# A layer norm taken in centred form: output weights and residual less their means

## The chip, the cores and the metric

The kernel runs on one core of a Trainium2 chip. The metric is the device time of one execution, in microseconds (us); the number that counts is the median over runs.

## The reference, cut to what matters

One post-norm decoder layer over 256 tokens and 1024 channels. Four mixers (Mamba-2 SSD, HGRN2, retention, block-sparse attention) of 256 channels each fill `y_cat`; one projection leads back to 1024 channels, and a layer norm with weight and bias ends it.

```python
def _layernorm(x, g, b):
    xf = x.astype(F32)
    mu = jnp.mean(xf, -1, keepdims=True)
    var = jnp.mean(jnp.square(xf - mu), -1, keepdims=True)
    return ((xf - mu) * lax.rsqrt(var + LN_EPS) * g + b).astype(x.dtype)
...
    y_cat = jnp.concatenate([y_ssd, y_hgrn, y_ret, y_moba], axis=-1).astype(x.dtype)
    y = jnp.einsum('blm,md->bld', y_cat, w_out)
    return _layernorm(DEEPNORM_ALPHA * x + y, ln_g, ln_b)
```

All of it is float32; the change touches only the last two lines.

## The kernel before, in words

**Tiles.** 256 tokens are two tiles of 128 (T = 0, 1). The contraction over 1024 channels is eight tiles of 128. Every matmul runs in a split form: a float32 operand is taken apart into a high part (rounded to the matmul's type) and a low part (the rest), and three products are added up: high by high, low by high, high by low. For weights `split_hi` (L225) makes the high part `whi` by a cast on ACT and `split_lo` (L234) the low part `wlo` by a subtraction on DVE.

**Slots.** The work is written by hand as a row of slots. Slots 0 to 29 are the input projections (`project`), two slots for a unit of 256 columns or for half of a pair of units. At slot s `begin(s)` starts the load of weight half s+6 (five buffers `raw`, all loads on SP's queue, in order), makes the high part of half s+4 on ACT, runs the steps that the table `steps` lists for that slot, and makes the low part of half s+4 on DVE. Every engine works its own instructions strictly in the order in which they are written. So ACT's and DVE's queues hold the weight splits between the mixers' steps.

**Output projection.** `w_out` is loaded as four blocks of 256 rows, each in two halves j of 512 columns (`wr_wo`; i = NU + 0 to 3, NU = 15, with `ORDER` = 0, 3, 1, 2: SSD, attention, HGRN2, retention). They are split in slots 26 to 33, four slots ahead of use. `oproj(i, T, c0, c1)` (L992 to L994) adds one block into a PSUM bank `po`. Its left side is `yhi`, `ylo`, the split of the transposed mixer outputs, made by `y_split` (L436 on ACT, L437 on DVE) and, for attention, L896 and L897. The order on PE: block 0 and block 1 for T = 0, the transposes of HGRN2 and retention (slot 32, L431), block 0 for T = 1, blocks 2 and 3 for T = 0, and at the end blocks 1 to 3 for T = 1, column piece by column piece. T = 0 has two pieces of 512 columns, T = 1 pieces of 512, 256, 256 (`OCOLS`).

**Slots 26 to 33 hold more than splits.** ACT makes the attention gate (`moba_out`, L894) and its `yhi`, the two SiLU gates of HGRN2 and retention from the last projection (`gates`, L630, slot 30) and the two `yhi` copies after the transposes (slot 32). POOL makes the retention norm's inverse root (`rsqrt_of`, L255 and L256: a multiply-add and a power).

**Residual.** `residual(T)` (slots 21, 22; L977, L978) puts alpha times the normalized input, with weight and bias, into `xn[T]`, on DVE. It reads the row vectors `rb`, whose one buffer is loaded again for the last norm's weight and bias once both residuals are through; SP issues the later weight loads behind that load.

**Last norm.** When a piece of `po` is complete, `out_add` adds it into `xn` (L1000) and takes statistics of the piece (L1001). After the last piece `out_norm` joins the statistics (L1006), has POOL make the inverse root (L255, L256), meanwhile subtracts the mean and multiplies by the weight (L1011), then multiplies by the root, adds the bias (L1014), and SP stores the pieces.

Of the kernel before, what the change touches and what calls it, by code (L numbers as in the profile page):

```python
# [122 lines left out]
def hybrid_layer(  # L123
# [21 lines left out]
    def sb(shape, name, tag=None, dt=F32, bufs=1):  # L145
        return sp.tile(shape, dt, name=name, tag=tag or name, bufs=bufs)
# [24 lines left out]
    mhalf = cp.tile([P, 8], F32, name="mhalf")  # L171
    nc.gpsimd.memset(mhalf, -0.5)


# [794 lines left out]
    def load_rows(first):  # L969
# [3 lines left out]
        rowt[first] = t  # L973

    def residual(T):
        rb = rowt[0]
        nc.vector.scalar_tensor_tensor(xn[T], xn[T], ALPHA, rb[:, 0, :], op0=ALU.mult, op1=ALU.mult)  # L977
        nc.vector.scalar_tensor_tensor(xn[T], rb[:, 1, :], ALPHA, xn[T], op0=ALU.mult, op1=ALU.add)  # L978

# [15 lines left out]

    fst = [sb([P, len(OCOLS[T]) - 1, 6], f"fst{T}") for T in range(NT)]

    def out_add(T, n):
        cs = slice(OCOLS[T][n], OCOLS[T][n + 1])
        nc.vector.tensor_add(xn[T][:, cs], xn[T][:, cs], po[T, cs.start])  # L1000
        nc.vector.bn_stats(fst[T][:, n, :], xn[T][:, cs])  # L1001

    def out_norm(T):
        rb = rowt[2]
        m_ = sb([P, 2], f"fmv{T}")
        nc.vector.bn_aggr(m_, fst[T])  # L1006
        rs = sb([P, 1], f"frs{T}")
        rsqrt_of(rs, m_[:, 1:2], 1.0, LN_EPS)
        cuts = [slice(a, b) for a, b in zip(OCOLS[T], OCOLS[T][1:])]
        for cs in (slice(0, 512), slice(512, 1024)):  # L1010
            nc.vector.scalar_tensor_tensor(xn[T][:, cs], xn[T][:, cs], m_[:, 0:1], rb[:, 0, cs],  # L1011
                                           op0=ALU.subtract, op1=ALU.mult)
        for cs in cuts:
            nc.vector.scalar_tensor_tensor(xn[T][:, cs], xn[T][:, cs], rs[:, 0:1], rb[:, 1, cs],  # L1014
                                           op0=ALU.mult, op1=ALU.add)
            nc.sync.dma_start(out[T * P:(T + 1) * P, cs], xn[T][:, cs])
# [45 lines left out]
    def begin(slot):  # L1062
        if slot < 32:
            load_w(*divmod(slot + 6, 2))
        if slot < 34:
            split_hi(*divmod(slot + 4, 2))
        for st in steps.get(slot, []):
            st()
        if slot < 34:
            split_lo(*divmod(slot + 4, 2))  # L1070

    first_unit()
# [62 lines left out]
```

## Time and profile before

| | us |
|---|---|
| median of 3 runs (lowest to highest) | 150.19 (150.09 to 150.38) |
| the profiled execution | 150.68 |
| its span, first to last instruction | 149.0 |
| PE busy, 1224 matmuls | 137.5 |
| DVE busy, 240 instructions | 116.5 |
| ACT busy, 122 instructions | 75.0 |
| POOL busy, 23 instructions | 17.8 |

The span is what the trace covers; 1.68 us of the profiled execution lie outside it. A busy share is a mean over stages with different limits, so it only says where to look first. The chain that ended last tells at each moment which instruction was waited for; an engine's timeline tells what ended its idle time (in brackets, with the releaser). The mean granted clock of TensorE was 0.971.

### The profile page before, as it was taken

Reading aid. Unit: us, or ns where it says so; the run is one execution under the profiler, and the core shown is the slowest. Engines: PE = TensorE matmul, PEld = TensorE weight load, DVE = VectorE, ACT = ScalarE, POOL = GpSimd, SP = SyncE. Lnnn points to the kernel's source line nnn. Section 1 sums busy time; section 2 is a strip of 40 time slices with the busy share of each in tenths; the row PEclk is TensorE's granted clock in tenths of the full one; section 3 lists DMA queues with packets and bytes.
Section 4 is the critical chain, followed back from the end, with each engine's and each line's share of the span. In section 5 each row is a group of like instructions: output and inputs, shape, how many; then the busy total and the mean of one; then the engine's idle time right before and its main releaser. Section 6 shows DMA issues by size and latency. Waiting matters only on the chain.

```text
span 149.0 us, 3073 instructions
## 1 busy us (share of the span) xinstructions
PE 137.5 (92%) x1224; PEld 122.5 (82%) x1224; DVE 116.5 (78%) x240; ACT 75.0 (50%) x122; POOL 17.8 (12%) x23
## 2 busy tenths in 40 slices
PE   5869999999999999999999999999999999999800
PEld 3149999999999998878899999999888888888800
DVE  1789968999596297969997599976989975478681
ACT  3088969742451759599709970054954635000000
POOL 4230000000000000000062018014004000004040
PEclk9996999999999999999999999999999999999975
DMA  4998399998748431595524830179774530000304
GB/s 141 328 384 312 95 292 342 324 319 317 201 139 258 136 60 80 148 272 165 163 101 145 306 119 4 35 232 383 243 239 141 159 127 0 0 0 0 141 0 141
DMA packets 9389, 26.05 MB, mean 175 GB/s; under 512 B 1056, under 2 KB 1696, under 8 KB 9120
## 3 DMA queue, kind: packets, MB, share of 16 engines
q1 hardware_dynamic: 9376, 25.87, 53.3%
q8 instruction: 9, 0.15, 0.4%
q14 instruction: 4, 0.03, 0.1%
HBM read 24.82 MB, written 1.05 MB: 174 GB/s over the span
## 4 chain that ended last, share of the span: by engine, by line
PE 81%; DVE 7%; DMA 3%; ACT 2%; SPq 1%; issue 1%; POOLq 1%; POOL 1%; DVEq 0%
PE pj_gg L381 8%; PE po L993 5%; PE po L994 5%; PE po L992 5%; PE pj_h_f L346 5%; PE pj_xs L420 4%; PE pj_m_k L420 4%; PE pj_m_g L420 4%; PE pj_r_k L420 4%; PE pj_m_q L420 4%; PE pj_h_i L420 4%; PE pj_zv L381 4%; PE pj_h_q L420 4%; PE pj_r_v L420 4%; PE pj_r_q L420 4%; DMA wr_h_f<-in_w_dram 3%
## 5 line engine op out<-in xcount | busy, mean ns | idle before, releaser
L992 PE MATMUL po<-whi_wo,yhi 128*128 128x512 f32 (+1 forms) x40 | 14.0, 350 | 0.0
L993 PE MATMUL po<-wlo_wo,yhi 128*128 128x512 f32 (+1 forms) x40 | 14.0, 349 | 0.0
L994 PE MATMUL po<-whi_wo,ylo 128*128 128x512 f32 (+1 forms) x40 | 13.9, 348 | 0.0
L234 DVE TENSOR_TENSOR wlo_wo<-wr_wo,whi_wo 128x1024 fp32r<-128x1024 f32 x8 | 9.6, 1219 | 0.0
L225 ACT CAST whi_wo<-wr_wo 128x1024 fp32r<-128x1024 f32 x8 | 8.2, 1050 | 2.3 <-PE pj_gg L381 1.7
L710 POOL TENSOR_SCALAR_AFFINE_SELECT ra<-ahi 128x1024 fp32r<-128x1024 f32 x1 | 1.1, 1101 | 65.0 <-DVE ahi L706 65.0
L992 PEld LDWEIGHTS po<-whi_wo,yhi 128*128 128x128 f32 x40 | 7.5, 188 | 1.1
L994 PEld LDWEIGHTS po<-whi_wo,ylo 128*128 128x128 f32 x40 | 7.5, 188 | 1.0
L993 PEld LDWEIGHTS po<-wlo_wo,yhi 128*128 128x128 f32 x40 | 7.5, 188 | 1.0
L225 ACT CAST whi_zv<-wr_zv 128x1024 fp32r<-128x1024 f32 x4 | 4.2, 1048 | 6.8 <-PE pj_xs L420 3.4
L179 PE MATMUL warm<-warm 128*128 128x512 f32 x6 | 5.5, 1088 | 1.5 <-DVE warm L176 1.5
L656 DVE SCALAR_TENSOR_TENSOR cacc_xs<-pj_xs,ch,cacc_xs 128x255 f32<-128x255 f32 (+2 forms) x6 | 2.9, 482 | 4.7 <-ACT cacc_xs L654 4.6
L381 PE MATMUL pj_zv<-whi_zv,hhi 128*128 128x512 f32 x16 | 6.5, 406 | 0.0
L381 PE MATMUL pj_gg<-whi_gg,hhi 128*128 128x512 f32 x16 | 6.4, 398 | 0.0
L1000 DVE TENSOR_TENSOR xn<-xn,po 128x512 f32<-128x512 f32 (+1 forms) x5 | 2.9, 580 | 4.4 <-PE po L994 4.4
L381 PE MATMUL pj_zv<-whi_zv,hlo 128*128 128x512 f32 x16 | 6.3, 394 | 0.0
L381 PE MATMUL pj_gg<-whi_gg,hlo 128*128 128x512 f32 x16 | 6.3, 394 | 0.0
L381 PE MATMUL pj_zv<-wlo_zv,hhi 128*128 128x512 f32 x16 | 6.3, 392 | 0.0
L381 PE MATMUL pj_gg<-wlo_gg,hhi 128*128 128x512 f32 x16 | 6.3, 392 | 0.0
L225 ACT CAST whi_gg<-wr_gg 128x1024 fp32r<-128x1024 f32 x4 | 4.2, 1046 | 2.5 <-DMA wr_gg<-in_w_dram 1.7
L793 ACT ACTIVATE ssq<-sy 128x512 f32<-128x512 f32 x1 | 0.6, 631 | 9.0 <-DVE sy L791 9.0
L860 ACT ACTIVATE pe<-pe,mmax 128x128 f32<-128x128 f32 (+1 forms) x8 | 3.5, 445 | 3.0 <-DVE mmax L853 3.0
(281 smaller groups left out, 494.1 us busy)
## 6 DMA issues: line engine op xcount, KB each, us to landing
wr_wo<-in_wo_dram SPq DMA_DIRECT2D x8, 512.0 KB, 3.9
wr_zv<-in_w_dram SPq DMA_DIRECT2D x4, 512.0 KB, 4.5
rb<-in_rows_dram SPq DMA_DIRECT2D x2, 1024.0 KB, 6.5
wr_gg<-in_w_dram SPq DMA_DIRECT2D x4, 512.0 KB, 4.9
wr_h_i<-in_w_dram SPq DMA_DIRECT2D x2, 520.0 KB, 5.3
xt<-in_x_dram SPq DMA_DIRECT2D x4, 256.0 KB, 3.7
wr_h_f<-in_w_dram SPq DMA_DIRECT2D x4, 256.0 KB, 5.0
wr_h_q<-in_w_dram SPq DMA_DIRECT2D x2, 512.0 KB, 6.7
```

The lines of the kernel that those rows point to most:

```text
L179: nc.tensor.matmul(wb, warm[:, :P], warm, start=True, stop=True)
L225: copy(whi[i, j][:, r, :], t[:, r, :])
L234: nc.vector.tensor_sub(wlo[i, j][:, r, :], t[:, r, :], whi[i, j][:, r, :].bitcast(F32))
L346: nc.tensor.matmul(ps[n], l[:, n * P:(n + 1) * P], r[:, k, :], start=(k == 0 and q == 0), stop=(k == KT - 1 and q == 2))
L381: nc.tensor.matmul(ps_of[name, T], l[:, k, ts], r, start=(k == 0 and q == 0), stop=(k == KT - 1 and q == 2))
L420: nc.tensor.matmul(ps, l, r, start=(n == 0), stop=(n == len(seq) - 1))
L656: nc.vector.scalar_tensor_tensor(a_[:, d:], ps[:, :SEQ - d], tap(3 - d), a_[:, d:], op0=ALU.mult, op1=ALU.add)
L860: nc.scalar.activation(pt[:, h, :], pt[:, h, :], AF.Exp, bias=mmax[:, i:i + 1], accum_out=msum[:, i:i + 1])
L992: nc.tensor.matmul(po[T, c0], yhi[:, k, ts], hi, start=(i == 0 and j == 0), stop=False)
L993: nc.tensor.matmul(po[T, c0], yhi[:, k, ts], lo, start=False, stop=False)
L994: nc.tensor.matmul(po[T, c0], ylo[:, k, ts], hi, start=False, stop=(i == 3 and j == 1))
L1000: nc.vector.tensor_add(xn[T][:, cs], xn[T][:, cs], po[T, cs.start])
```

## The change

The mean over the 1024 output channels of alpha x + y is taken out of the inputs of the sum. Each row of `w_out` (one input channel, one partition) gets its mean over the 1024 columns subtracted before it is split, and the residual gets its own row mean subtracted. The sum then has row mean zero. The variance is the mean of squares, and the weight can be applied before the inverse root is known.

- `residual(T)`: the second instruction also gives its row sum; a one-column multiply on DVE; ACT adds the negative mean to the whole row.
- `wo_sum`, in the place of `split_hi` for the output weights: ACT copies each of a half's two row tiles in place, for the accumulator's row sum (two passes of 512 columns).
- `wo_mean`, after the second half of a block: POOL adds the two halves' sums and multiplies by -1/1024.
- `wo_split`, in odd slots after the steps, for both halves at once: ACT makes the high parts with the mean as bias (four passes of 512), DVE the low parts (four instructions).
- `out_add`: after the add ACT squares the piece, with an accumulator, and writes the squares over the spent bank; DVE multiplies the piece by the weight into `zg` and joins the piece's sum to the variance.
- `out_norm`: one POOL power, then the last multiply-add from `zg`.

```diff
--- before.py
+++ after.py
@@ -170,6 +170,8 @@
 
     mhalf = cp.tile([P, 8], F32, name="mhalf")
     nc.gpsimd.memset(mhalf, -0.5)
+    epsln = cp.tile([P, 1], F32, name="epsln")
+    nc.gpsimd.memset(epsln, LN_EPS)
 
 
     warm = sb([P, 512], "warm", tag="att")
@@ -972,10 +974,43 @@
         nc.sync.dma_start(t, rows[:, o:o + 2 * DM].to_broadcast([P, 2 * DM]))
         rowt[first] = t
 
+
+
     def residual(T):
         rb = rowt[0]
         nc.vector.scalar_tensor_tensor(xn[T], xn[T], ALPHA, rb[:, 0, :], op0=ALU.mult, op1=ALU.mult)
-        nc.vector.scalar_tensor_tensor(xn[T], rb[:, 1, :], ALPHA, xn[T], op0=ALU.mult, op1=ALU.add)
+        sm_ = sb([P, 1], f"rsum{T}")
+        nc.vector.scalar_tensor_tensor(xn[T], rb[:, 1, :], ALPHA, xn[T], op0=ALU.mult, op1=ALU.add,
+                                       accum_out=sm_)
+        nc.vector.tensor_scalar(sm_, sm_, -1.0 / DM, None, op0=ALU.mult)
+        nc.scalar.activation(xn[T], xn[T], AF.Identity, bias=sm_[:, 0:1])
+
+    wsum = sb([P, 2, 8], "wsum")
+
+    def wo_sum(i, j):
+        for q in range(2):
+            o = 2 * (i - NU) + q
+            nc.scalar.activation(raw[i, j][:, q, :], raw[i, j][:, q, :], AF.Copy,
+                                 accum_out=wsum[:, j, o:o + 1])
+
+    def wo_mean(i):
+        m = 2 * (i - NU)
+        wm = wsum[:, 0, m:m + 2]
+        nc.gpsimd.tensor_tensor(wm, wm, wsum[:, 1, m:m + 2], op=ALU.add)
+        nc.gpsimd.tensor_scalar(wm, wm, -1.0 / DM, None, op0=ALU.mult)
+
+    def wo_split(i):
+
+        wm = wsum[:, 0, 2 * (i - NU):2 * (i - NU) + 2]
+        for j in range(2):
+            whi[i, j] = part_tile(i, j, "whi", SPENT_HI)
+            wlo[i, j] = part_tile(i, j, "wlo", SPENT_LO)
+            for q in range(2):
+                nc.scalar.activation(whi[i, j][:, q, :], raw[i, j][:, q, :], AF.Identity,
+                                     bias=wm[:, q:q + 1])
+                nc.vector.scalar_tensor_tensor(wlo[i, j][:, q, :], raw[i, j][:, q, :], wm[:, q:q + 1],
+                                               whi[i, j][:, q, :].bitcast(F32),
+                                               op0=ALU.add, op1=ALU.subtract)
 
 
     po = {}
@@ -993,25 +1028,32 @@
             nc.tensor.matmul(po[T, c0], yhi[:, k, ts], lo, start=False, stop=False)
             nc.tensor.matmul(po[T, c0], ylo[:, k, ts], hi, start=False, stop=(i == 3 and j == 1))
 
-    fst = [sb([P, len(OCOLS[T]) - 1, 6], f"fst{T}") for T in range(NT)]
+    zg = [[sb([P, 512], f"zg{T}{n}", tag=(("sy", "ho"), ("xdt", "xsd"))[T][n]) for n in range(2)]
+          for T in range(NT)]
+    fss = [sb([P, 3], f"fss{T}") for T in range(NT)]
+    fvar = [sb([P, 1], f"fvar{T}") for T in range(NT)]
+
+    def zpart(T, n):
+        c0, c1 = OCOLS[T][n], OCOLS[T][n + 1]
+        return zg[T][c0 // 512][:, c0 % 512:c0 % 512 + c1 - c0]
+
+    def out_var(T, n):
+        nc.vector.scalar_tensor_tensor(fvar[T], fss[T][:, n:n + 1], 1.0 / DM,
+                                       epsln if n == 0 else fvar[T], op0=ALU.mult, op1=ALU.add)
 
     def out_add(T, n):
         cs = slice(OCOLS[T][n], OCOLS[T][n + 1])
         nc.vector.tensor_add(xn[T][:, cs], xn[T][:, cs], po[T, cs.start])
-        nc.vector.bn_stats(fst[T][:, n, :], xn[T][:, cs])
+        nc.scalar.activation(po[T, cs.start], xn[T][:, cs], AF.Square, accum_out=fss[T][:, n:n + 1])
+        nc.vector.tensor_mul(zpart(T, n), xn[T][:, cs], rowt[2][:, 0, cs])
+        out_var(T, n)
 
     def out_norm(T):
-        rb = rowt[2]
-        m_ = sb([P, 2], f"fmv{T}")
-        nc.vector.bn_aggr(m_, fst[T])
         rs = sb([P, 1], f"frs{T}")
-        rsqrt_of(rs, m_[:, 1:2], 1.0, LN_EPS)
-        cuts = [slice(a, b) for a, b in zip(OCOLS[T], OCOLS[T][1:])]
-        for cs in (slice(0, 512), slice(512, 1024)):
-            nc.vector.scalar_tensor_tensor(xn[T][:, cs], xn[T][:, cs], m_[:, 0:1], rb[:, 0, cs],
-                                           op0=ALU.subtract, op1=ALU.mult)
-        for cs in cuts:
-            nc.vector.scalar_tensor_tensor(xn[T][:, cs], xn[T][:, cs], rs[:, 0:1], rb[:, 1, cs],
+        nc.gpsimd.tensor_tensor(rs, fvar[T], mhalf[:, :1], op=ALU.pow)
+        for n, (a, b) in enumerate(zip(OCOLS[T], OCOLS[T][1:])):
+            cs = slice(a, b)
+            nc.vector.scalar_tensor_tensor(xn[T][:, cs], zpart(T, n), rs[:, 0:1], rowt[2][:, 1, cs],
                                            op0=ALU.mult, op1=ALU.add)
             nc.sync.dma_start(out[T * P:(T + 1) * P, cs], xn[T][:, cs])
 
@@ -1062,12 +1104,18 @@
     def begin(slot):
         if slot < 32:
             load_w(*divmod(slot + 6, 2))
-        if slot < 34:
+        if slot < 26:
             split_hi(*divmod(slot + 4, 2))
+        elif slot < 34:
+            wo_sum(*divmod(slot + 4, 2))
+            if slot % 2:
+                wo_mean((slot + 4) // 2)
         for st in steps.get(slot, []):
             st()
-        if slot < 34:
+        if slot < 26:
             split_lo(*divmod(slot + 4, 2))
+        elif slot < 34 and slot % 2:
+            wo_split((slot + 4) // 2)
 
     first_unit()
     lower_bound()
```

On ACT, from the first half of output block 2 (named wo1) on, before. `wr` is the loaded half, `whi` its high part, `gg` the gates, `yhi` the copies after the transposes `yt1` and `yt2`:

```order
L225 CAST whi_wo1_0_1595<-wr_wo1_0_1556 128x1024
L630 ACTIVATE gg_182<-pj_gg0_1503 128x512
L630 ACTIVATE gg_182<-pj_gg1_1510 128x512
L225 CAST whi_wo1_1_1618<-wr_wo1_1_1575 128x1024
L225 CAST whi_wo2_0_1635<-wr_wo2_0_1593 128x1024
L436 CAST yhi_170<-yt1_1637 128x512
L436 CAST yhi_170<-yt2_1642 128x512
L225 CAST whi_wo2_1_1667<-wr_wo2_1_1616 128x1024
```

The same place in the changed kernel, where `wsum` holds the sums and then the mean:

```order
L993 ACTIVATE wr_wo1_0_1581,wsum_219<-wr_wo1_0_1581 128x512 x2
L632 ACTIVATE gg_184<-pj_gg0_1516 128x512
L632 ACTIVATE gg_184<-pj_gg1_1523 128x512
L993 ACTIVATE wr_wo1_1_1598,wsum_219<-wr_wo1_1_1598 128x512 x2
L1009 ACTIVATE whi_wo1_0_1656<-wr_wo1_0_1581,wsum_219 128x512 x2
L1009 ACTIVATE whi_wo1_1_1662<-wr_wo1_1_1598,wsum_219 128x512 x2
L993 ACTIVATE wr_wo2_0_1628,wsum_219<-wr_wo2_0_1628 128x512 x2
L438 CAST yhi_172<-yt1_1682 128x512
L438 CAST yhi_172<-yt2_1687 128x512
L993 ACTIVATE wr_wo2_1_1649,wsum_219<-wr_wo2_1_1649 128x512 x2
L1009 ACTIVATE whi_wo2_0_1714<-wr_wo2_0_1628,wsum_219 128x512 x2
L1009 ACTIVATE whi_wo2_1_1720<-wr_wo2_1_1649,wsum_219 128x512 x2
```

Ahead of the two `yhi` copies there now stand all eight passes of wo1 and two of wo2, where two casts and half a block stood; the high parts of a block come only after both its halves' sums.

On POOL, from the retention norm to the end, before (`rrs`: the retention norm's root; `frs`: the last norm's, for each T):

```order
L255 TENSOR_SCALAR rrs<-rmv 128x8
L256 TENSOR_TENSOR rrs<-rrs,mhalf 128x8
L255 TENSOR_SCALAR frs_1708<-fmv_1706 128x1
L256 TENSOR_TENSOR frs_1708<-frs_1708,mhalf 128x1
L255 TENSOR_SCALAR frs_1779<-fmv_1777 128x1
L256 TENSOR_TENSOR frs_1779<-frs_1779,mhalf 128x1
```

And in the changed kernel:

```order
L999 TENSOR_TENSOR wsum<-wsum 128x2
L1000 TENSOR_SCALAR wsum<-wsum 128x2
L257 TENSOR_SCALAR rrs<-rmv 128x8
L258 TENSOR_TENSOR rrs<-rrs,mhalf 128x8
L999 TENSOR_TENSOR wsum<-wsum 128x2
L1000 TENSOR_SCALAR wsum<-wsum 128x2
L999 TENSOR_TENSOR wsum<-wsum 128x2
L1000 TENSOR_SCALAR wsum<-wsum 128x2
L999 TENSOR_TENSOR wsum<-wsum 128x2
L1000 TENSOR_SCALAR wsum<-wsum 128x2
L1053 TENSOR_TENSOR frs_1765<-fvar_226,mhalf 128x1
L1053 TENSOR_TENSOR frs_1837<-fvar_227,mhalf 128x1
```

Four pairs for the means are new, one of them ahead of the retention norm's root, and the last norm's pairs are down to one instruction each.

On DVE, the last norm of T = 1, before (`fst`: statistics, `fmv`: mean and variance):

```order
L1000 TENSOR_TENSOR xn_111<-xn_111,po_768_1671 128x256
L1001 BN_STATS fst_218<-xn_111 128x6
L1006 BN_AGGR fmv_1777<-fst_218 128x2
L1011 SCALAR_TENSOR_TENSOR xn_111<-xn_111,fmv_1777,rb_1301 128x512 x2
L1014 SCALAR_TENSOR_TENSOR xn_111<-xn_111,frs_1779,rb_1301 128x512
L1014 SCALAR_TENSOR_TENSOR xn_111<-xn_111,frs_1779,rb_1301 128x256 x2
```

And in the changed kernel, from the same add on (`fss`: the sums of squares):

```order
L1046 TENSOR_TENSOR xn_113<-xn_113,po_768_1726 128x256
L1048 TENSOR_TENSOR zg_223<-xn_113,rb_1316 128x256
L1041 SCALAR_TENSOR_TENSOR fvar_227<-fss_225,fvar_227 128x1
L1056 SCALAR_TENSOR_TENSOR xn_113<-zg_222,frs_1837,rb_1316 128x512
L1056 SCALAR_TENSOR_TENSOR xn_113<-zg_223,frs_1837,rb_1316 128x256 x2
```

The two instructions of statistics and the two wide multiplies are gone from behind the last add; a 256-wide multiply and a one-column step stand there.

## Rows read from the trace of the kernel before

**Rows 1.** The page's part 1: busy us, share of the span, instructions.

```profile
PE 137.5 (92%) x1224; PEld 122.5 (82%) x1224; DVE 116.5 (78%) x240; ACT 75.0 (50%) x122; POOL 17.8 (12%) x23
```

**Rows 2.** The chain that ended last, in order: start us, us, what.

```profile
106.63 11.27 PE pj_gg L381 x48
...
123.47 0.87 PE yt L431 x8
...
127.14 0.23 PE po L992
...
132.68 0.24 PE po L992
...
140.97 0.13 PE po L994
...
141.12 0.43 DVE xn L1000
...
143.15 1.00 POOLq L1131
...
144.18 0.75 DVE xn L1014
```

**Rows 3.** ACT's timeline from 98 us: start, us, instruction, shape [idle before <-releaser].

```profile
98.66 0.63 ACT L793 ACTIVATE ssq<-sy 128x512 f32<-128x512 f32 x1 [9.03 <-DVE sy L791]
...
104.34 1.05 ACT L225 CAST whi_wo<-wr_wo 128x1024 fp32r<-128x1024 f32 x1 [0.35 <-DMA wr_wo<-in_wo_dram]
...
109.50 0.62 ACT L896 CAST yhi<-mo 128x512 fp32r<-128x512 f32 x1 [1.72 <-DVE mo L895]
...
123.94 1.07 ACT L436 CAST yhi<-yt 128x512 fp32r<-128x512 f32 x2 [3.50 <-PE yt L431]
124.90 1.07 ACT L225 CAST whi_wo<-wr_wo 128x1024 fp32r<-128x1024 f32 x1
```

**Rows 4.** ACT's timeline: passes of 512, 256, and 256 with bias column and accumulator.

```profile
9.26 0.60 ACT L225 CAST whi_h_f<-wr_h_f 128x512 fp32r<-128x512 f32 x1
9.77 0.56 ACT L311 ACTIVATE hhi<-tr,ch 128x256 fp32r<-128x256 f32 x1
...
14.74 0.41 ACT L316 CAST hhi<-hf 128x256 fp32r<-128x256 f32 x1
...
63.57 0.19 ACT L860 ACTIVATION_READ_ACCUMULATOR pe<-pe,mmax 128x1 f32 x1
63.67 0.50 ACT L860 ACTIVATE pe<-pe,mmax 128x256 f32<-128x256 f32 x1
64.07 0.19 ACT L860 ACTIVATION_READ_ACCUMULATOR pe<-pe,mmax 128x1 f32 x1
```

**Rows 5.** DVE's timeline: an instruction of a few columns.

```profile
54.49 0.17 DVE L853 TENSOR_SCALAR mmax<-mmax 128x4 f32<-128x4 f32 x1
```

**Rows 6.** POOL's timeline: its multiply-adds and powers of a few columns.

```profile
6.81 0.57 POOL L271 TENSOR_TENSOR lrs<-lrs,mhalf 128x1 f32<-128x1 f32 x1
...
88.88 1.10 POOL L255 TENSOR_SCALAR hrs<-hss 128x8 f32<-128x8 f32 x1 [9.88 <-DVE hss L618]
...
113.67 0.20 POOL L255 TENSOR_SCALAR rrs<-rmv 128x8 f32<-128x8 f32 x1 [11.37 <-DVE rmv L959]
```

**Rows 7.** DVE's timeline beside those POOL steps, and a pair of 512-wide instructions.

```profile
88.71 1.21 DVE L977 SCALAR_TENSOR_TENSOR xn<-xn,rb 128x1024 f32<-128x1024 f32 x1
...
113.62 0.69 DVE L960 TENSOR_TENSOR ro<-reo,rmv 128x512 f32<-128x512 f32 x1
...
142.31 1.42 DVE L1011 SCALAR_TENSOR_TENSOR xn<-xn,fmv,rb 128x512 f32<-128x512 f32 x2
```

**Rows 8.** The page's part 6, DMA issues: KB each, median us to landing.

```profile
wr_wo<-in_wo_dram SPq DMA_DIRECT2D x8, 512.0 KB, 3.9
```

**Rows 9.** By stretch of us: PE, PEld, DVE, ACT, POOL busy, PEclk, DMA share, GB/s.

```profile
6.00:8.00 2.00, 0.99 (x2) 0.00 (x0) 1.90 (x7) 0.00 (x0) 1.18 (x3) 1.00 1.02 353
...
10.00:12.00 2.00, 1.62 (x8) 1.60 (x8) 1.77 (x7) 2.00 (x5) 0.29 (x1) 0.62 1.02 391
```

## The prediction

> **What bounds the kernel now.** I read the busy shares first: TensorE (PE) is busy 92% of the span, VectorE (DVE) 78, ScalarE (ACT) 50, GpSimd (POOL) 12 [rows 1]. Next the chain that ended last, in order of time [rows 2]. From 106.63 to 141.10 us it is PE matmuls alone: the gate projection to 117.90, the output projection up to the transposes at 123.47, output block 2 from 127.14, the last blocks of token tile 1 from 132.68 to 141.10 (8.42 us that need nothing new from another engine). Then PE is done and the last layer norm runs as a chain: add, statistics, the two POOL steps, and the last multiply-add, which starts at 144.18, 3.08 us after PE's end. From there to the end of the span it is 4.82 us, for the stores too. So there are two places to win or lose: PE's gap-free stretch, and the 3.08 us behind it. A reader should see in the third view, ACT's own timeline [rows 3], why the first of these is delicate: today ACT has only eight 1.05 us casts to make for the output weights, the first at 104.34 us, the last at 124.90, and it waits in between (1.72 us for DVE before the `yhi` copy at 109.50, 3.50 us for PE before the two `yhi` copies at 123.94).
>
> **What the change takes off the end.** The statistics, their aggregation and one POOL step go; in their place ACT squares the 256 new columns with an accumulator, DVE adds the sum to the variance, POOL takes the power. Step by step: the add stays, 0.43 us [rows 2]; a 256-wide ACT pass 0.40 up to the accumulator read and 0.19 for that [rows 4]; a one-column DVE instruction 0.17 [rows 5]; the power 0.57 where DVE was not in its way [rows 6], against the 1.00 of today, when DVE's multiply stood beside it [rows 2]; five hand-overs of about 0.05 (from POOL's end at 144.15 to DVE's start 0.03 in [rows 2]). That is about 2.0 us instead of 3.08: **1.1 us won**. The multiply by the weight hides under the ACT pass. The final multiply-adds and stores are the same sizes, so 4.82 us stay.
>
> **What it adds in front.** The residual: two one-column DVE instructions of 0.17 [rows 5] and two accumulator reads; I take 0.5 us on DVE. The two new 1024-wide ACT passes cost nothing there: ACT is idle for 9.03 us before its square at 98.66 [rows 3], and they run in that hole, with the two casts of `gg` weights that now stand behind them. The DVE delay does reach the second load of row vectors, which waits for the residual, and with it the weight loads queued on SP behind it, about 0.25 us. And it reaches the `yhi` copy that waits for DVE: 110.0 instead of 109.50 [rows 3]. PE feels perhaps 0.15 us of it.
>
> The output weights are the large part. Today each half block costs ACT one cast of 1.05 us. Now it costs two sum passes and two subtracting passes of 512 columns. A plain 512-wide pass takes 0.60 and the next starts 0.51 later; an accumulator read adds 0.10; a bias from a column costs 0.09 more (0.50 against 0.41 at 256 columns) [rows 4]. So a sum pass takes **0.62** of the queue and a subtracting pass **0.61 to 0.62**. Per block that is 8 passes, 5.0 us, where it was 2.1.
>
> Then the wait. A block's four subtracting passes need the mean, and the mean is made on POOL from all four sums. ACT works strictly in order, so it stands still for: the accumulator's write (0.1), the hand-over (0.1), a POOL add, 0.08, a POOL multiply, 0.05. The multiply has a row at 0.20; the add has none of its own: it lies between 0.20 and the power's 0.57, and 1.10 is what a POOL step took when DVE blocked it [rows 6]. I take 0.30 and 0.22, since at these four moments DVE has run out of work that blocks POOL (the low parts wait for the very passes that wait for POOL; at the first one DVE is at its statistics from PSUM). So a gap of **0.85 us, four times**. Behind ACT stand, in its queue, the two SiLU gates and the two `yhi` copies that PE needs. On POOL the first mean stands ahead of the retention norm's root, which today runs at 113.67 [rows 6]; the mean is through by then or shortly after, and what waits for the root is wanted only at PE's transposes at 123. On DVE, in out_add, the variance step waits for ACT and the next columns' add stands behind it; in token tile 0 that costs some tenths long before PE is done.
>
> The sum of ACT's queue from 110.0 us: up to the first `yhi` copy of output blocks 1 and 2 there are the moba copy (0.53), 12 sum passes (7.4), 12 subtracting passes (7.4), three gaps (2.55) and two gates (1.0): 18.9, so the copy starts at 128.9 and is done at **129.5**; today it starts at 123.94 [rows 3]. PE meanwhile loses some 0.5 us at the transposes, because the gates come out at 123 and DVE must still multiply twice, and it reaches block 2 at about 127.8. It then stands for 1.7 us. After the copies (1.0) come two more sums (1.25) and the fourth gap (0.85): the first high part of the last block is there at 132.8, DVE follows with four low parts at 0.67 each (two of a like form took 1.42 [rows 7]), so the last low part is there at **135.6**. PE needs 0.5 more for the two matmuls behind it, then its 8.42 us: it ends at **144.5** instead of 141.10.
>
> Does the load of weights suffer? A buffer is free only after its low part; the latest, freed at about 120.5, lands 3.9 us later [rows 8] at 124.5 and is wanted at 130. No.
>
> The span: 144.5 + 2.0 + 4.8 = **151.3 us, 2.3 more than 149.0**. The profiled execution took 150.68 in all, 1.68 outside the span; the median of the runs is 150.19, 0.49 below it. On the median: 150.19 + 2.3 = **152.5 us**. The centred form wins a third of what the ACT queue costs.
>
> **Rivals.**
>
> *The gaps are longer: POOL is blocked.* POOL's step at 88.88 took 1.10 us and ended when DVE's multiply with two SBUF inputs (88.71, 1.21) did; the same step at 113.67 took 0.20 beside a DVE instruction that read PSUM (113.62) [rows 6, 7]. The low parts have two SBUF inputs. If two POOL steps of each mean took 1.10, each gap would grow by 1.7, PE's end by 6.8, and the time would be near 159; if only the add costs 0.57, it is 1.1 more, 153.6. Against it: the order leaves DVE nothing of that kind to do just then. The Trainium skill (SBUF — State Buffer, section Who interferes with whom) has the rule for it: a VectorE instruction with two SBUF inputs and a GpSimd instruction that reads SBUF exclude each other for the whole of the one that came first. By that rule the means would be free here, and blocked as soon as a low part ran beside them; the two rows agree with it, and no row shows a POOL add.
>
> *PE's clock falls in the new hole.* After the warm-up matmuls PE was busy 0.99 of 2 us, and sparsely up to 10 us; from 10 to 12 the granted clock was 0.62, that is partly at the lower level [rows 9]. The new hole is of that order, 1.7 us. If the clock fell for as long as it did there, some three us at half speed, it would cost 1.5 us: 154. For it: the rows. Against it: around the hole PE is full, which it was not there.
>
> *The cover holds and the end decides: faster.* If bias column and accumulator read were hidden behind the streaming, a pass would take 0.51, and if both POOL steps took 0.20, the 26 passes and four gaps before the last high part would shrink by 2.8 and 0.5. PE would then end at 141.2, bounded by its own work again, the 1.1 us of the end would be won, and the time would be 149.3. It turns at 2.3 us, 0.09 per pass. Against it: the accumulator reads in [rows 4] lie back to back with the passes and hide nothing.
>
> *The change does nothing measurable*: the same with half of that saving, 150.2. Nothing speaks for just that.
>
> **The numbers.** Forecast (ACT's queue with POOL's gaps sets PE's end, 151.6 to 153.6): 0.60. Longer gaps: 0.15. Clock: 0.13. Faster: 0.07. No change: 0.05. Faster and same, and the far end of the blocked case, are left outside; the range is bounded below by passes 0.03 us cheaper and POOL steps of 0.20 (1.4 less, 151.1, and 0.5 for what I may have overlooked: 150.6) and above by the clock or gaps longer by 0.6 each (155). This kernel's measurement can tell about 0.2%, 0.3 us, from no change: faster 0.07, same 0.05, slower 0.88.
>
> **What would show it.** Right: in the after trace ACT is busy or waiting for POOL without other holes from 110 to 134; the two `yhi` copies start near 129; PE has a hole of one to two us before block 2, waiting for ACT; PE ends near 144.5; the last multiply-add starts 2.0 us behind it. Wrong in size: passes not at 0.62, or POOL's add far from 0.3. Wrong in kind: PE without holes after 118, or a wait for weights from DMA, or a longer chain behind PE's end because ACT's square starts late.

## The result, and the profile after

The changed kernel takes 152.74 us in the median of four runs (151.7 to 152.87), the kernel before 150.28 beside it: a ratio of 1.014, with a 95% interval of 1.0102 to 1.0178. It is slower by 2.5 us where the prediction had 2.3; two repetitions, below, gave 1.020 and 1.014. The profiled execution took 152.87 us, with a span of 151.2 where the prediction had 151.3. An agreement to 0.1 us says little by itself: two terms may be wrong by the same amount. One run each of e6, of e7 and of the kernel before in the first set below was over 1.5% longer than the fastest of its kernel; medians and ranges there are of the other runs.

The busy shares come first (busy us, share of the span, instructions; against [rows 1]):

```profile
PE 138.6 (92%) x1224; PEld 122.2 (81%) x1224; DVE 115.9 (77%) x251; ACT 92.3 (61%) x174; POOL 17.4 (11%) x30
```

PE has the same 1224 matmuls. ACT went from 75.0 to 92.3 us with 52 more instructions. Neither says where the time went: ACT is still idle for 39% of the span. That is read from ACT's own timeline (start, us, instruction, shape, and in brackets the idle time before it and what ended it), against [rows 3]:

```profile
105.98 0.63 ACT L993 ACTIVATE wr_wo<-wr_wo 128x512 f32<-128x512 f32 x1 [1.87 <-DMA wr_wo<-in_wo_dram]
...
109.09 0.60 ACT L896 ACTIVATE g_m_g<-pj_m_g 128x512 f32<-128x512 f32 x1
110.45 0.62 ACT L898 CAST yhi<-mo 128x512 fp32r<-128x512 f32 x1 [0.76 <-DVE mo L897]
...
112.95 2.56 ACT L1009 ACTIVATE whi_wo<-wr_wo,wsum 128x512 fp32r<-128x512 f32 x4 [0.64 <-POOL wsum L1000]
115.42 0.62 ACT L993 ACTIVATE wr_wo<-wr_wo 128x512 f32<-128x512 f32 x1
...
116.03 0.62 ACT L993 ACTIVATE wr_wo<-wr_wo 128x512 f32<-128x512 f32 x1
...
117.26 0.62 ACT L993 ACTIVATE wr_wo<-wr_wo 128x512 f32<-128x512 f32 x1
117.78 0.19 ACT L993 ACTIVATION_READ_ACCUMULATOR wr_wo<-wr_wo 128x1 f32 x1
118.59 2.57 ACT L1009 ACTIVATE whi_wo<-wr_wo,wsum 128x512 fp32r<-128x512 f32 x4 [0.62 <-POOL wsum L1000]
...
125.18 2.56 ACT L1009 ACTIVATE whi_wo<-wr_wo,wsum 128x512 fp32r<-128x512 f32 x4 [0.61 <-POOL wsum L1000]
...
128.87 1.04 ACT L438 CAST yhi<-yt 128x512 fp32r<-128x512 f32 x2
...
131.76 2.57 ACT L1009 ACTIVATE whi_wo<-wr_wo,wsum 128x512 fp32r<-128x512 f32 x4 [0.61 <-POOL wsum L1000]
```

From the moba copy at 110.45 to the last block's high parts ACT has no hole but four, one ahead of each block's subtracting passes, each ended by POOL. The sum passes start every 0.61 to 0.62 us. A fifth pass behind the fourth (117.26) would have started at 117.88; the high parts start at 118.59, so a gap costs 0.71 us. The two `yhi` copies start at 128.87, where in [rows 3] they started at 123.94 after a wait for PE. Now PE waits for them. These are PE's matmuls that had to wait, the one ahead of the last wait, and the last matmul (same columns):

```profile
124.21 0.63 PE L433 MATMUL yt<-ck,ho 128*128 128x128 f32 x4 [0.77 <-DVE ho L636]
...
129.49 0.50 PE L1027 MATMUL po<-whi_wo,yhi 128*128 128x512 f32 x1 [1.30 <-ACT yhi L438]
...
132.64 0.40 PE L1027 MATMUL po<-whi_wo,yhi 128*128 128x512 f32 x1
133.33 0.50 PE L1028 MATMUL po<-wlo_wo,yhi 128*128 128x512 f32 x1 [0.29 <-DVE wlo_wo L1011]
...
144.28 0.28 PE L1029 MATMUL po<-whi_wo,ylo 128*128 128x256 f32 x1
```

The same matmuls in the kernel before (the transposes, block 2's first, the last):

```profile
123.30 0.60 PE L431 MATMUL yt<-ck,ho 128*128 128x128 f32 x4
...
126.97 0.39 PE L992 MATMUL po<-whi_wo,yhi 128*128 128x512 f32 x1
...
140.81 0.28 PE L994 MATMUL po<-whi_wo,ylo 128*128 128x256 f32 x1
```

PE ends at 144.56, 3.46 us later than in [rows 2]. The starts tell where: the transposes are 0.91 later, block 2 another 1.61, and the last matmul another 0.95. About half of that last part lies where PE waits for the first low part of the last block (0.69 from start to start, 132.64 to 133.33, where 0.23 is usual). Behind PE's end the chain is the new one (DVE and POOL, same columns):

```profile
144.60 0.42 DVE L1046 TENSOR_TENSOR xn<-xn,po 128x256 f32<-128x256 f32 x1 [0.96 <-PE po L1029]
...
145.83 0.56 POOL L1053 TENSOR_TENSOR frs<-fvar,mhalf 128x1 f32<-128x1 f32 x1 [6.82 <-DVE fvar L1041]
...
146.43 1.54 DVE L1056 SCALAR_TENSOR_TENSOR xn<-zg,frs,rb 128x512 f32<-128x512 f32 x3 [0.67 <-POOL frs L1053]
```

The final multiply-add starts 1.87 us after PE's end; it was 3.08 in [rows 2]. So the end won 1.2 us and the front lost 3.5.

### The profile page after: what moved, and what is told of

The parts are those of the page before. It is cut to its first block, busy times and chain, and to the rows that moved or that the text cites. A ratio compares the mean times of both kernels' runs of the same rounds, so it can differ in the third digit from the quotient of the medians.

```text
span 151.2 us, 3148 instructions
## 1 busy us (share of the span) xinstructions
PE 138.6 (92%) x1224; PEld 122.2 (81%) x1224; DVE 115.9 (77%) x251; ACT 92.3 (61%) x174; POOL 17.4 (11%) x30
## 5 line engine op out<-in xcount | busy, mean ns | idle before, releaser
L1011 DVE SCALAR_TENSOR_TENSOR wlo_wo<-wr_wo,wsum,whi_wo 128x512 fp32r<-128x512 f32 x16 | 11.0, 747 | 5.0 <-ACT whi_wo L1009 5.0
L1009 ACT ACTIVATE whi_wo<-wr_wo,wsum 128x512 fp32r<-128x512 f32 x16 | 10.3, 712 | 2.5 <-POOL wsum L1000 2.5
L993 ACT ACTIVATE wr_wo<-wr_wo 128x512 f32<-128x512 f32 x16 | 9.9, 620 | 1.9 <-DMA wr_wo<-in_wo_dram 1.9
L1047 ACT ACTIVATE po<-xn 128x512 f32<-128x512 f32 (+1 forms) x5 | 2.6, 517 | 8.0 <-DVE xn L1046 8.0
L986 ACT ACTIVATE xn<-xn,rsum 128x1024 f32<-128x1024 f32 x2 | 2.3, 1155 | 6.9 <-DVE rsum L985 6.9
```

Source lines behind the costliest of these rows:

```text
L993: nc.scalar.activation(raw[i, j][:, q, :], raw[i, j][:, q, :], AF.Copy, accum_out=wsum[:, j, o:o + 1])
L1009: nc.scalar.activation(whi[i, j][:, q, :], raw[i, j][:, q, :], AF.Identity, bias=wm[:, q:q + 1])
L1011: nc.vector.scalar_tensor_tensor(wlo[i, j][:, q, :], raw[i, j][:, q, :], wm[:, q:q + 1], whi[i, j][:, q, :].bitcast(F32), op0=ALU.add, op1 ...
L1047: nc.scalar.activation(po[T, cs.start], xn[T][:, cs], AF.Square, accum_out=fss[T][:, n:n + 1])
```

## The experiments

Twelve runs followed (two of them the changed kernel again), in three sets of four (in the table's order: four, then e8, e7, e6, e5, then the last four). Each set ran on one chip beside the kernel before (150.11, 150.33 and 150.49 us there), to which its ratios are taken. The ratios are those on record and differ from the quotient of the two medians by up to 0.3%. "Copy" is the start of the moba copy (`yhi<-mo`) in the profiled run, "last" that of PE's last matmul.

| kernel | median us (range) | ratio to before [95%] | copy | last | last less copy |
|---|---|---|---|---|---|
| before | 150.28 (150.09 to 150.77) | | 109.50 | 140.81 | 31.31 |
| changed | 152.74 (151.7 to 152.87) | 1.014 [1.0102, 1.0178] | 110.45 | 144.28 | 33.83 |
| e1_weights_old | 148.74 (148.5 to 148.97) | 0.9906 [0.9874, 0.9938] | 109.67 | 140.17 | 30.50 |
| e2_tail_old | 153.83 (153.26 to 154.7) | 1.0251 [1.019, 1.0312] | 109.64 | 143.45 | 33.81 |
| e3_no_mean_wait | 149.86 (149.18 to 150.73) | 0.9982 [0.995, 1.0015] | 109.61 | 140.66 | 31.05 |
| e4_yhi_first | 151.94 (151.63 to 152.23) | 1.012 [1.0082, 1.0158] | 109.77 | 143.55 | 33.78 |
| e8_after_again | 152.94 (152.35 to 153.28) | 1.0198 [1.0166, 1.0231] | 109.92 | 143.75 | 33.83 |
| e7_mean_twice | 154.96 (153.72 to 155.64) | 1.0313 [1.0262, 1.0364] | 109.79 | 146.34 | 36.55 |
| e6_residual_old | 151.56 (151.36 to 152.19) | 1.0108 [1.0073, 1.0144] | 109.79 | 143.60 | 33.81 |
| e5_mean_hidden | 149.85 (149.06 to 150.88) | 0.9978 [0.995, 1.0006] | 109.78 | 141.21 | 31.43 |
| e12_after_five | 152.6 (151.66 to 153.02) | 1.0144 [1.011, 1.0178] | 110.01 | 143.85 | 33.84 |
| e9_sum_behind_gate | 151.85 (151.29 to 152.92) | 1.0108 [1.0072, 1.0144] | 109.53 | 143.35 | 33.82 |
| e11_gate_residual_old | 151.84 (151.27 to 152.05) | 1.0089 [1.0055, 1.0122] | 109.48 | 143.32 | 33.84 |
| e10_hidden_behind_gate | 149.7 (149.08 to 150.88) | 0.9956 [0.9931, 0.998] | 109.67 | 141.04 | 31.37 |

**The change cut in two.** One kernel splits the output weights as before and keeps the new residual and last norm (its sum is not centred, so it serves for timing only); the other keeps the centred weights and residual and has the last norm of before.

```diff
-        if slot < 26:
+        if slot < 34:
             split_hi(*divmod(slot + 4, 2))
-        elif slot < 34:
-            wo_sum(*divmod(slot + 4, 2))
...
```

```diff
-        nc.scalar.activation(po[T, cs.start], xn[T][:, cs], AF.Square, accum_out=fss[T][:, n:n + 1])
-        nc.vector.tensor_mul(zpart(T, n), xn[T][:, cs], rowt[2][:, 0, cs])
-        out_var(T, n)
+        nc.vector.bn_stats(fst[T][:, n, :], xn[T][:, cs])
...
```

> The output weights are split as before (one cast and one subtraction per half, no sums, no mean); residual and end of the norm stay as changed. The weights keep their means, so the sum is not centred. Theory (ACT's queue with sums and POOL's means costs the time, the end of the norm wins some): PE ends where it did before plus 0.2 us, the end stays 1.2 us shorter, 149.2 us, ratio 0.993. Rival (the end of the norm wins nothing on the chip, or the residual's extra work costs): 150.3 or more.

> Centred weights and residual as changed, but the last norm taken as before (statistics on DVE, two POOL steps, two wide multiplies). Theory: PE ends at 144.6 as in the changed kernel and the old end of 7.9 us follows: 153.9 us, ratio 1.024. Rival (the end costs the same in either form): 152.7.

Both came near the theory (e1 0.5 us below its 149.2): 1.4 us won without the weights' part, 3.7 lost without the new end, together 2.35, where the whole change cost 2.5. This is not a clean split: both kernels keep the new residual, so the sum counts it twice. In the first PE again runs without a hole from 117 us, and the final multiply-add starts 1.86 us after PE's end (142.31 less 140.45); in the second it starts 3.09 after it (146.82 less 143.73). The end's gain is the same with or without the loss in front.

**What the gaps cost.** This kernel makes the sums and the means and takes the bias from a column of zeros, so no pass waits for POOL (its weights are not centred).

```diff
+    zcol = cp.tile([P, 2], F32, name="zcol")
+    nc.gpsimd.memset(zcol, 0.0)
...
-        wm = wsum[:, 0, 2 * (i - NU):2 * (i - NU) + 2]
+        wm = zcol
```

> As changed, with sums and POOL's means still made, but the bias of the high and low parts comes from a column of zeros set at the start, so that nothing waits for a mean; the weights are not centred. Theory: the four gaps of 0.62 us on ACT close, PE ends 2.5 us earlier, 150.2 us. Rival 1 (DVE's low parts, at 0.67 each, set the pace and take the place of the gaps): 151.5 to 152.7. Rival 2 (the passes are not what binds, the gaps are all of it): below 149.5.

It gave 149.86, no slower than the kernel before, and from the moba copy to PE's last matmul 31.05 us instead of 33.83: 2.78 less, where four gaps of 0.71 make 2.84. So the four waits stand on the path one for one. All 32 passes are still made; against the eight casts of e1 they cost 0.55 on this stretch (31.05 against 30.50). The waits, not the passes, are the larger part of the loss.

The opposite test gives POOL two more steps in each mean.

```diff
         nc.gpsimd.tensor_scalar(wm, wm, -1.0 / DM, None, op0=ALU.mult)
+        nc.gpsimd.tensor_scalar(wm, wm, 2.0, None, op0=ALU.mult)
+        nc.gpsimd.tensor_scalar(wm, wm, 0.5, None, op0=ALU.mult)
```

> The changed kernel with two more multiplies on POOL in each mean (by 2, then by 0.5, so the value is the same): each of the four gaps in ACT's queue grows by two POOL steps of 0.29 from start to start, 0.58 us. Theory (all four gaps stand in the row of work that ends in PE's last matmul, so each counts one for one): 2.3 us more, 155.0 us; PE's hole ahead of output block 2 grows from 1.30 to 3.0 us, and the one ahead of the last block's low part stays about 0.3 to 0.9. Rival (the first gaps are swallowed by ACT's waits for other engines or by PE's slack, and only one or two of them reach the end): 0.6 to 1.2 us more, 153.3 to 153.9.

It gave 154.96, 2.0 us above the changed kernel in the same set, against 2.3 by the theory and 0.6 to 1.2 by the rival. Each of ACT's four waits grew to 1.20 to 1.23 us, 0.59 more, 2.36 in all, and all four count. But from copy to last matmul it is 2.72 more. The other 0.36 us are in PE's windows (busy us of PE, PEld, DVE, ACT, POOL, then granted clock, DMA share, GB/s), for this kernel:

```profile
128.00:130.00 2.00, 0.69 (x6) 0.49 (x5) 1.78 (x3) 2.00 (x7) 0.00 (x0) 1.00 0.00 0
130.00:132.00 2.00, 1.41 (x5) 0.84 (x6) 1.29 (x2) 2.00 (x6) 0.00 (x0) 0.94 0.00 0
132.00:134.00 2.00, 2.00 (x6) 1.61 (x5) 0.00 (x0) 0.80 (x3) 0.83 (x4) 0.50 0.00 0
134.00:136.00 2.00, 2.00 (x8) 1.55 (x8) 1.79 (x3) 2.00 (x4) 0.00 (x0) 0.71 0.00 0
136.00:138.00 2.00, 2.00 (x10) 1.67 (x9) 1.97 (x4) 0.43 (x2) 0.00 (x0) 1.00 0.00 0
```

and in its matmuls there (columns as before):

```profile
130.59 0.50 PE L1029 MATMUL po<-whi_wo,yhi 128*128 128x512 f32 x1 [1.90 <-ACT yhi L438]
...
132.41 0.63 PE L1031 MATMUL po<-whi_wo,ylo 128*128 128x512 f32 x1
132.84 0.63 PE L1029 MATMUL po<-whi_wo,yhi 128*128 128x512 f32 x1
133.26 0.63 PE L1030 MATMUL po<-wlo_wo,yhi 128*128 128x512 f32 x1
...
135.52 0.39 PE L1030 MATMUL po<-wlo_wo,yhi 128*128 128x512 f32 x1
135.75 0.39 PE L1031 MATMUL po<-whi_wo,ylo 128*128 128x512 f32 x1
```

After a hole of 1.90 us (and one of 1.19 at the transposes) the granted clock went to 0.50, the level of 1.2 GHz, about a microsecond after PE had started again, and came back near 135: start to start 0.43 us instead of 0.23. This is the rival of the falling clock. Little of what it cost reached the end, since PE would have waited in part of that time: DVE starts the last block's low parts at 134.21 here, and in the changed kernel the first matmul on them started 0.81 behind that (132.52 to 133.33); by that it would have been 135.02, and it was 135.52, 0.50 later. From there to the last matmul it is 10.82 us, in the changed kernel, where PE had stood still just before, 10.95; that leaves about 0.37. In the changed kernel's own windows the clock is 1.00 through its hole of 1.30 us:

```profile
128.00:130.00 2.00, 0.70 (x4) 0.30 (x2) 1.21 (x3) 2.00 (x7) 0.00 (x0) 1.00 0.00 0
130.00:132.00 2.00, 2.00 (x9) 1.48 (x9) 0.76 (x2) 1.39 (x5) 0.41 (x2) 1.00 0.00 0
132.00:134.00 2.00, 1.71 (x8) 1.00 (x7) 1.48 (x3) 2.00 (x4) 0.00 (x0) 1.00 0.00 0
```

The Trainium skill (TensorE: Matmul & The Clock Gate, section Wait — 56ns, not 53.3ns?) has 426.7 ns from start to start for 512 columns on the slow clock, and the rows agree (seven starts from 132.41 to 134.97, 0.427 apart). For the fast clock it has 215.7 ns; here it is 0.23 us, and the measurement decides.

**Which wait of PE binds.** In this kernel the two `yhi` copies stand ahead of the last block's first sums, so that PE gets them 1.2 us sooner (17.18 us behind the moba copy instead of 18.42).

```diff
-            wo_sum(*divmod(slot + 4, 2))
+            if slot != 32:
+                wo_sum(*divmod(slot + 4, 2))
...
+        if slot == 32:
+            wo_sum(*divmod(slot + 4, 2))
```

> As changed, but on ACT the two yhi copies stand ahead of the last block's first two sums. Nothing is left out. Theory (the last block's parts at the end of ACT's queue set PE's end, PE's hole before block 2 is only where that shows first): the hole of 1.3 us closes to 0.1, PE waits as much longer for the last block, 152.7 us, ratio to the kernel before 1.015 as it was. Rival (the hole before block 2 is the loss itself): 1.2 us less, 151.5.

The time, 151.94, lies between the two, nearer to the rival's, and its interval overlaps that of the changed kernel. The trace decides: the hole of 1.30 us at the copies is gone (0.34 for DVE's `ylo` stands there), and PE waits for the last block's high and low parts instead:

```profile
131.85 0.49 PE L1027 MATMUL po<-whi_wo,yhi 128*128 128x512 f32 x1 [0.62 <-ACT whi_wo L1009]
132.63 0.50 PE L1028 MATMUL po<-wlo_wo,yhi 128*128 128x512 f32 x1 [0.29 <-DVE wlo_wo L1011]
```

From copy to last matmul it is 33.78 us, as in the changed kernel (33.83). What binds is the whole of ACT's queue up to the last block's first high part; the hole of 1.30 us was only the place where PE stood.

**The residual.** This kernel has the residual of before.

```diff
-        nc.vector.scalar_tensor_tensor(xn[T], rb[:, 1, :], ALPHA, xn[T], op0=ALU.mult, op1=ALU.add,
-                                       accum_out=sm_)
-        nc.vector.tensor_scalar(sm_, sm_, -1.0 / DM, None, op0=ALU.mult)
-        nc.scalar.activation(xn[T], xn[T], AF.Identity, bias=sm_[:, 0:1])
+        nc.vector.scalar_tensor_tensor(xn[T], rb[:, 1, :], ALPHA, xn[T], op0=ALU.mult, op1=ALU.add)
```

> The changed kernel with the residual of before: no row sum in DVE's multiply-add, no scaling of it, no 1024-wide subtracting pass on ACT. What it leaves out: the residual keeps its row mean, so the last norm lacks that part of the centring; all sizes are the same. Theory (the residual's work lies in holes of DVE and ACT, and reaches the end only by the yhi copy of the moba part, a few tenths): 0 to 0.3 us less than the changed kernel, 152.4 to 152.7. Rival (its DVE time holds up the weight loads behind it on the DMA queue, and these the sums; the first sum waited 1.87 us for its load): 0.7 us less or more, 152.0 or below.

It gave 151.56, 1.4 less than the changed kernel in the same set (the intervals do not overlap): by the times the theory was wrong, and the number is the rival's. From copy to last matmul nothing changed (33.81), so the gain must lie ahead of the copy. The two profiled executions show little of it: the copy starts at 109.79 against 109.92 in e8, and they took 152.19 (the longest of e6's three) and 152.35 (the shortest of e8's four). So the size stays open here. In the changed kernel ACT waits 1.87 us for the first output weights, ahead of the gate from which the moba product and the copy are made; with the old residual the first sum starts at once:

```profile
104.68 0.63 ACT L989 ACTIVATE wr_wo<-wr_wo 128x512 f32<-128x512 f32 x1
...
109.79 0.62 ACT L898 CAST yhi<-mo 128x512 fp32r<-128x512 f32 x1 [1.39 <-DVE mo L897]
```

To tell the late load from the residual's own work, the next two kernels move the first two sum passes behind that gate, with the new and with the old residual.

```diff
         nc.scalar.activation(g, ps_of["m_g"], AF.Silu)
+        wo_sum(15, 0)
...
```

> The changed kernel with one move in ACT's order: the first two sum passes, which waited 1.87 us for their weights, stand behind the moba gate's SiLU instead of ahead of the transposed copy, the table load and that SiLU. Theory A (the late landing of the first weights holds up the gate, and with it the moba copy from which ACT's queue runs without a break): the gate is out two microseconds earlier, the moba product then waits only for DVE's own queue, the moba copy starts at about 109.8 instead of 110.45 us where the gate projection starts at 106.5, and as the end hangs on that copy the time falls by 0.4 to 0.7 us, to 152.0 to 152.3 or 1.010 to 1.014. Theory B (the moba copy is bound by DVE and the projection in any case, the wait for the load lies in slack): no change, 152.7. Theory C (the two passes now stand in the row itself): up to 0.6 us more.

> The same move together with the residual of before (left out: the centring of the residual; its row mean stays in, and all sizes are the same). Theory A (the centred residual costs time only because the first weights land later behind it, which the move makes harmless): within 0.3 us of the kernel with the move alone. Rival (the centred residual costs some 0.5 to 1 us by DVE's own time ahead of the gate projection, wherever the weights land): 0.5 to 1 us less than the kernel with the move alone.

> The changed kernel once more, as the mark for the three that follow on the same chip: 152.7 us, 1.014 to 1.020 of the kernel before. In all profiled runs so far that had the centred residual and this order, ACT's first sum waited 1.5 to 1.9 us for the load of its weights; the same is expected here.

The move gave 151.85 against 152.6 for the unchanged order (the intervals overlap), and with the move the old residual gave 151.84, no difference. In the profiled executions of this set trace and time agree: the copy is 0.48 (e9) and 0.53 us (e11) sooner than in e12, and the times are 0.50 and 0.52 shorter (151.94 and 151.92 against 152.44). This supports theory A: the centred residual costs time only where the weights behind it land late and ACT waits for them ahead of the gate. In e9 the gate starts some 2 us earlier than in e12 (106.48 against 108.65) and the copy waits for DVE alone:

```profile
106.48 0.60 ACT L896 ACTIVATE g_m_g<-pj_m_g 128x512 f32<-128x512 f32 x1
...
109.53 0.62 ACT L899 CAST yhi<-mo 128x512 fp32r<-128x512 f32 x1 [1.23 <-DVE mo L898]
```

Why the load lands late is open. The seven other profiled runs with the new residual and the sums (or casts) ahead of the gate waited 1.30 to 1.89 us for it, the kernel before 0.35, e6 nothing; but the next kernel, e5, has the new residual too and waited 0.18. In four traces (before, changed, e5, e6) the first of these loads was issued at 96.2 to 96.5 us, so it was not the issue that differed; nor was it the amount moved, since from 96 to 104 us the DMA rates add up to 2.26 MB both in the changed kernel and in e5.

**A version that beats both.** The four gaps go if ACT has something to do while POOL makes the mean. This kernel keeps every instruction and changes only the order on ACT, and with it that of the low parts on DVE: a block's second sums, the next block's first sums, and only then the block's subtracting passes. At the end the `yhi` copies come ahead of the third block's subtracting passes, and the last block's second sums stand between the two halves of these.

```diff
...
+        elif slot < 34 and slot % 2:
+            i = (slot + 4) // 2
+            wo_sum(i, 1)
+            wo_mean(i)
+            if i < 18:
+                wo_sum(i + 1, 0)
...
+        elif slot in (27, 29):
             wo_split((slot + 4) // 2)
+        elif slot == 32:
+            wo_split(17, (0,))
+        elif slot == 33:
+            wo_split(17, (1,))
+            wo_split(18)
```

> Same instructions and same result as the changed kernel; only ACT's order is another: each block's second sums are made, then the next block's first sums, and only then the block's subtracting passes, so that POOL makes each mean while ACT works. For the last block the two yhi copies lie behind its first sums and the first half of the block before it. Theory (the four gaps at the mean are what costs most, 0.7 us each, and go one for one into PE's end): PE's last matmul ends 35.3 to 36.0 us after the gate projection's first matmul (38.0 in the changed kernel, 35.5 where nothing waited for a mean), and the time is 149.8 us, 0.4 less than the kernel before. Rival (the twelve passes ahead of the yhi copies bind by their own length, and the order only moves the wait elsewhere): 37 or more, and 151 us or more.

> The changed kernel itself once more, beside the three that follow, so that they are compared on one chip. Both theories: 152.7 us, 1.014 of the kernel before; PE's last matmul ends 38.0 us after its first matmul of the gate projection (the changed kernel's trace: 106.54 to 144.56).

> The means hidden behind the next block's sums, and the first two sums behind the moba gate: same result as the changed kernel, only ACT's order differs. With hidden means ACT still has no slack at the yhi copies (they waited 0.25 us for PE), so by theory A up to 0.5 us less than with hidden means alone wherever the first weights land late: 149.4 us, 0.993 to 0.997 of the kernel before. By theory B the same as with hidden means alone: 149.85, 0.998.

With hidden means it is 149.85, 3.1 us less than the changed kernel in the same set and as fast as the kernel in which nothing waited for a mean (0.9978 and 0.9982). From the gate projection's first matmul to PE's end it is 34.97 us (106.52 to 141.49), a little under the 35.3 to 36.0 expected. With the first sums behind the gate as well it is 149.7, 0.9956 of the kernel before [0.9931, 0.998]: faster by about 0.4%. What the second move adds (0.15 us between the medians, of different chips) can't be told from nothing. ACT's rows in that last kernel have no wait for POOL:

```profile
112.66 2.55 ACT L1010 ACTIVATE whi_wo<-wr_wo,wsum 128x512 fp32r<-128x512 f32 x4
...
117.57 2.55 ACT L1010 ACTIVATE whi_wo<-wr_wo,wsum 128x512 fp32r<-128x512 f32 x4
...
123.74 1.08 ACT L438 CAST yhi<-yt 128x512 fp32r<-128x512 f32 x2 [0.21 <-PE yt L433]
124.70 1.35 ACT L1010 ACTIVATE whi_wo<-wr_wo,wsum 128x512 fp32r<-128x512 f32 x2
...
127.17 3.78 ACT L1010 ACTIVATE whi_wo<-wr_wo,wsum 128x512 fp32r<-128x512 f32 x6
```

The copies wait for PE again, as in [rows 3], and the chain that ended last, in its profile page, belongs to PE once more:

```profile
PE 71%; DVE 11%; issue 6%; ACT 5%; DMA 3%; POOL 1%; SPq 1%; POOLq 0%; DVEq 0%; ACTq 0%
```

## Why the prediction was right, step by step

*The end.* 1.1 us were forecast, 1.21 came (3.08 to 1.87); e1 and e2 give the same with and without the front. The steps were priced right in sum.

*The passes.* 0.62 and 0.61 to 0.62 us were forecast; the rows have 0.61 to 0.62 for the sums and 2.56 for four subtracting passes and their drain. The accumulator reads and the bias column are paid in full, as [rows 4] said.

*The gaps.* 0.85 us were forecast, 0.71 came: POOL's add took 0.20 us, not 0.30, its multiply 0.21 to 0.24. Four of them make 0.56 us less. They are on the path, one for one (e3, e7), as the prediction had them.

*The moba copy.* Forecast at 110.0, it came at 110.45 (109.92 and 110.01 in e8 and e12, where the gate projection began 0.7 us earlier and at the same time). The step that failed is the residual's "about 0.25 us" on the loads. The issue was late by about that much (the first output weights at 96.41 us against 96.23), but the weights landed 1.64 later (105.98 against 104.34), and the step left out that ACT's wait for them stands ahead of the gate. So a wait for weights from DMA, which the prediction lists as a sign of being wrong in kind, did occur, ahead of the stretch it had in mind. What it is worth is known only roughly: 0.13 to 0.53 us by the copy's start in e6, e9 and e11 against e8 and e12, 0.75 to 1.4 by the medians. The copy 0.45 too late and three gaps 0.42 too short in all cancelled, by luck; that is why the `yhi` copies came at 128.87 against a forecast of 128.9.

*PE's wait.* The transposes lost 0.91 us where 0.5 was forecast. The hole ahead of block 2 was forecast at 1.7 us from 127.8 and is 1.30 from 128.19. After it the prediction let the last low part decide (135.6, then 0.5 and 8.42). The trace has another: PE waits for the first low part (133.33) and then runs to its end without a break, the last low part (DVE's four end at 135.26) being there in time. By the forecast's rule that 135.26 would have given 144.2; PE's own matmuls from 133.33 give the 144.56 that was seen. So the agreement of PE's end with 144.5 is luck in this step too; the mechanism, ACT's queue with POOL's gaps, is what e3, e5 and e7 bear out.

*Two sums.* The prediction's case of no change is not half of the saving of the rival before it: 150.2 needs 2.3 of the 3.3 us. And 26 passes 0.03 cheaper with POOL steps of 0.20 save 1.3, not 1.4. Neither touches the forecast; the second moves the lower bound by 0.1.

*The rivals.* POOL was not blocked: its eight steps took 0.20 to 0.24 us, with DVE out of instructions with two SBUF inputs at those moments (at the third the last one ended 0.02 us into the add), as the prediction argued from the order. In e5 one mean did fall beside one (DVE's row, then POOL's):

```profile
116.17 0.69 DVE L966 TENSOR_TENSOR ro<-ro,rrs 128x512 f32<-128x512 f32 x1
```

```profile
116.62 0.29 POOL L999 TENSOR_TENSOR wsum<-wsum 128x2 f32<-128x2 f32 x1 [1.88 <-ACT wr_wo L993]
```

The add took 0.29 instead of 0.20 and ended at 116.91, just behind DVE's 116.86. The Trainium skill (SBUF — State Buffer, section Who interferes with whom) has the two exclude each other, and these rows agree. In e10 the same add took 0.29 again. The clock did not fall with a hole of 1.30 us (behind one of 0.77), and did with 1.90 in e7 (behind one of 1.19), so the forecast's hole of 1.7 lay between the two. The time of the rival in which the cover holds, 149.3, is nearly that of e10 (149.7), but not by its mechanism: the passes there still take 0.61 us each, and what went are the four gaps.

## What to carry to other kernels

A round trip to another engine can cost the engine that waits its whole length, and everything that stands in its queue behind it: here, where ACT had no slack behind the wait, 0.71 us four times, of which 0.41 is work on POOL. Before a reduction is given to a second engine, give the first something that doesn't need the result; the same instructions in another order were worth 3 us. And when a queue is full from some instruction to the end, look for what starts that instruction: a wait ahead of it can move the end just as one behind it does.

## What the runs showed that was not expected

With more work in the means the granted clock fell to 0.50 from about 131.7 to 135 us, a microsecond after PE had come out of a hole of 1.90 us (with one of 1.19 shortly before) and was full again; holes of 0.77 and 1.30 us left it at 1.00.

The time from the moba copy to the start of PE's last matmul was 33.78 to 33.84 us in all eight profiled runs in which each mean was one add and one multiply that ACT waited for. The times of the runs of one kernel spread by 0.5 to 1.9 us, so a stretch between two rows of the trace decided here what medians left open.
